# Even attention: probabilities times values as three products of high and low parts

## The chip, the cores and the metric

The kernel runs on one core of one Trainium2 chip. The metric is the device time of one execution in microseconds. Before the change it is 2157.37 us in the median of three runs (2157.3 to 2157.92).

## What is computed

The reference is one step of a two-layer trunk over 128 context and 512 latent tokens, with a width of 2048. Layer 0, the even one, has a windowed attention of 8 heads of 128 (two key and value heads) beside a gated linear attention (GLA); layer 1 has a neighbourhood attention beside a spatial gating. Each layer scales and shifts its input by a modulation that a conditioning vector gives, and adds its projected output through a gate. The change is in the latent tokens' attention of layer 0:

```python
s_band = einsum('bnqkgd,bnjkd->bnkgqj', qb, kb) * scale          # 3 blocks of 128 keys around a block
s_ctx = einsum('bnqkgd,blkd->bnkgql', qb, ck) * scale            # 128 cached keys
p = softmax(concatenate([s_band, s_ctx, sk], axis=-1), axis=-1)  # sk: a sink logit
...
o = einsum('bnkgqj,bnjkd->bnqkgd', pb, vb) + einsum('bnkgql,blkd->bnqkgd', pc, cv)
```

and in the modulation that the prediction speaks of:

```python
shift, scale, gate = split(silu(cond) @ ada_w[l] + ada_b[l], 3)
h = rms_norm(x, norm_g[l]) * (1.0 + scale) + shift
```

## The kernel before

**Tiling.** Activations lie with features on the 128 partitions, 16 tiles (k) of 640 tokens. A weight chunk of 128 output features is multiplied with all 16 tiles in two halves of the tokens (320 columns; 322 where two columns for the shift lie ahead). Weights and activations are split into a high part (fp32r, made by an ACT copy) and a low part (the rest, by a subtraction on POOL or DVE), and a product is three single-pass matmuls: high by high, low by high, high by low (`mm_k`). Small products (scores, transposes, probabilities by values, the GLA) are fp32 matmuls.

**Order.** The program is recorded by a planner. Its main list (`acts`) runs weight chunks; between matmuls `tick` (L454) advances tasks (generators such as `even_head`, L1389) whose inputs `Pace`, a model of the engines' times, holds to be ready. `Pace.record` (L138) books each instruction on its engine behind what it waits for. A low-priority task, `ada_task` (L1077), works off 640 reductions on DVE, each the product of 128 rows of a modulation matrix with the conditioning row: first 128 for the gate of layer 0, then 256 for scale and shift of layer 1 (written to `part`), and 256 half as long for the gate of layer 1 (to `partg`). `tick` adds one only where DVE, by the planner's clock, is not ahead of the present by more than `room` (0.3 us up to the end of the attention, then 1.5), and not in a `kpair` (L735) while any task is open. `need` lets the planner's time pass, without matmuls, until a flag is set.

**The stages around the change.** After the GLA, `open_att` (L1989) lays out the attention's buffers; then come chunks for k, v and q, and for each head a task `even_head`: rotary, five blocks of scores (`s1`), softmax (`soft1`, `soft2`), transposes of the probabilities and their copy from PSUM into `pT` (`s3`), and the product with the values into one bank. The attention's temporary buffers are parts of one tile, `arena`. `tok_major` (L1324) transposes the values. Gate chunks stand between heads. After the last head (`open_g0`, L2056) come two gate chunks, and the projection of layer 0 (`out_proj`, L2076). Its last two chunks are a `kpair`. After it `to_odd` (L2101) makes layer 1's input tile by tile: it waits for the flag `ada_1` that the 384th reduction sets. `rstd1` (L2119) makes the norm, and the main list has `need("shift1")` ahead of layer 1's first chunks.

## Time and profile before

| | |
|---|---|
| median of three runs | 2157.37 us |
| span of the profiled execution | 2155.7 us |
| TensorE busy, matmuls | 2099.9 us, 14326 |
| DVE busy | 1320.2 us |
| ACT busy | 907.2 us |
| POOL busy | 944.9 us |

The page has no own time of the profiled execution beside its span; the median lies 1.7 us above the span. Nearly all instructions go through helpers, so that lines tell little: matmuls have L371, transposes L376, and what DVE, ACT and POOL do has L205. Groups are told by the names and shapes of what they write and read. The attention runs from about 500 to 830 us, the projection of layer 0 from 883 to 1082 us, and layer 1 begins there.

### The profile page before, as it was taken

How to read it: one execution, taken by the hardware profiler on the slowest of the kernel's cores; microseconds unless marked ns; L12 is line 12 of the kernel's file. 1: busy time of each engine (PE TensorE's matmuls, PEld its weight loads, DVE VectorE, ACT ScalarE, POOL GpSimd, SP SyncE). 2: the span in 40 equal slices, each digit the busy share in tenths (PEclk: the TensorE clock that was granted, in tenths of full speed). 3: DMA queues.
4: the chain of work that ended last, by engine and by line, in shares of the span. 5: the costliest groups of instructions: out<-in, count | busy, mean ns of one | idle time of the engine just before them, and what ended most of it. 6: DMA issues, size and time to landing. Idle time of an engine off the chain costs nothing.

```text
span 2155.7 us, 38542 instructions
## 1 busy us (share of the span) xinstructions
PE 2099.9 (97%) x14326; PEld 2029.6 (94%) x14326; DVE 1320.2 (61%) x3190; ACT 907.2 (42%) x1962; POOL 944.9 (44%) x731
## 2 busy tenths in 40 slices
PE   7999999999999999999999999999999999999997
PEld 4789999999989999999999999999999999999996
DVE  1337787777777665889767887874344443354335
ACT  4435444343343444433464333444444453343333
POOL 3433333233223222566544455544444445536663
PEclk9999999999999999999999999999999999999998
DMA  9934433346435332577634345532222232233325
GB/s 374 365 136 153 133 103 105 105 126 192 124 98 165 128 123 81 193 226 220 212 99 127 119 139 163 185 103 79 89 78 78 88 134 80 80 109 122 105 93 193
DMA packets 161372, 303.08 MB, mean 141 GB/s; under 512 B 17376, under 2 KB 54048, under 8 KB 161184
## 3 DMA queue, kind: packets, MB, share of 16 engines
q1 hardware_dynamic: 159712, 299.06, 42.8%
q8 instruction: 112, 1.84, 0.3%
q10 hardware_dynamic: 1472, 1.56, 0.2%
q14 instruction: 76, 0.62, 0.1%
HBM read 278.52 MB, written 19.42 MB: 138 GB/s over the span
## 4 chain that ended last, share of the span: by engine, by line
PE 85%; DVE 5%; DMA 4%; issue 2%; POOL 2%; ACT 2%; SPq 0%; ACTq 0%; DVEq 0%; POOLq 0%
PE bank L371 82%; PE bank L376 2%; PE bank L1199 1%; DVE Y L205 1%; POOL wlo L205 1%; DMA rs<-w_out 1%; DVE arena L205 1%; DVE adas L205 1%; DMA adas<-ada 1%; ACT arena L205 1%; DVE bank L205 0%; ACT whi L205 0%; SPq L403 0%; DVE rs L205 0%; DMA crow<-crow 0%
## 5 line engine op out<-in xcount | busy, mean ns | idle before, releaser
L371 PE MATMUL bank<-acth,whi 128*128 128x320 f32 (+2 forms) x3592 | 1106.6, 318 | 18.2 <-DVE sums L205 8.8
L371 PE MATMUL bank<-acth,wlo 128*128 128x320 f32 (+2 forms) x3592 | 1078.6, 310 | 0.0
L371 PE MATMUL bank<-actl,whi 128*128 128x320 f32 (+2 forms) x3592 | 1077.3, 310 | 0.0
L205 POOL TENSOR_TENSOR wlo<-wraw,whi 128x512 fp32r<-128x512 f32 x375 | 504.2, 1348 | 724.2 <-ACT whi L205 634.0
L371 PEld LDWEIGHTS bank<-acth,whi 128*128 128x128 f32 (+1 forms) x3592 | 668.8, 189 | 35.5 <-DVE sums L205 10.3
L371 PEld LDWEIGHTS bank<-actl,whi 128*128 128x128 f32 (+1 forms) x3592 | 668.9, 189 | 1.5
L371 PEld LDWEIGHTS bank<-acth,wlo 128*128 128x128 f32 (+1 forms) x3592 | 668.4, 189 | 0.0
L205 POOL TENSOR_TENSOR wlo<-rs,whi 128x512 fp32r<-128x512 f32 x259 | 352.1, 1369 | 308.4 <-ACT whi L205 293.0
L205 ACT ACTIVATE whi<-wraw 128x512 fp32r<-128x512 f32 x383 | 237.0, 625 | 251.2 <-PE bank L371 116.0
L205 DVE TENSOR_TENSOR rs<-rs 128x512 f32<-128x512 f32 x148 | 155.2, 1050 | 134.0 <-DMA rs<-w_odd 57.8
L205 DVE CUSTOM_DVE_ANT_0 adas<-adas,bank,partg 128x256 bf16<-128x256 f32 (+1 forms) x320 | 178.6, 558 | 12.7 <-ACT bank L205 3.5
L205 ACT ACTIVATE whi<-rs 128x512 fp32r<-128x512 f32 x259 | 156.4, 621 | 27.3 <-PE bank L371 14.7
L205 DVE CUSTOM_DVE_ANT_0 adas<-adas,bank,part 128x512 bf16<-128x512 f32 x192 | 143.0, 745 | 9.7 <-ACT bank L205 3.6
L205 DVE TENSOR_TENSOR bank<-bank,sums 128x320 f32<-128x320 f32 (+1 forms) x148 | 72.4, 497 | 120.9 <-PE bank L371 120.2
L371 PE MATMUL bank<-eh,whi 128*128 128x322 f32 (+1 forms) x444 | 139.9, 315 | 0.0
L371 PE MATMUL bank<-el,whi 128*128 128x322 f32 (+1 forms) x444 | 137.6, 310 | 0.0
L371 PE MATMUL bank<-eh,wlo 128*128 128x322 f32 (+1 forms) x444 | 137.6, 310 | 0.0
L205 ACT ACTIVATE arena<-Y 128x320 f32<-128x320 f32 (+1 forms) x76 | 38.8, 512 | 172.7 <-DVE Y L205 152.8
L205 ACT ACTIVATE arena<-arena,bc 128x128 f32<-128x128 f32 (+4 forms) x171 | 84.9, 520 | 58.0 <-DVE arena L205 55.8
L205 ACT ACTIVATE bc<-bank 128x2 f32<-128x2 f32 (+1 forms) x101 | 17.2, 170 | 201.1 <-DVE arena L205 120.9
L205 POOL TENSOR_TENSOR arena<-arena 128x320 f32<-128x320 f32 x58 | 53.6, 924 | 103.8 <-ACT arena L205 103.2
L205 ACT ACTIVATE Y<-bank 128x128 f32<-128x128 f32 (+5 forms) x130 | 50.9, 410 | 110.4 <-PE bank L371 85.7
(159 smaller groups left out, 2215.5 us busy)
## 6 DMA issues: line engine op xcount, KB each, us to landing
wraw<-w_even SPq DMA_DIRECT2D x176, 256.0 KB, 3.2
adas<-ada_g SPq DMA_DIRECT2D x128, 256.0 KB, 3.7
adas<-ada SPq DMA_DIRECT2D x128, 256.0 KB, 3.6
wraw<-w_odd SPq DMA_DIRECT2D x124, 256.0 KB, 3.1
rs<-w_odd SPq DMA_DIRECT2D x50, 512.0 KB, 4.1
wraw<-w_out SPq DMA_DIRECT2D x88, 256.0 KB, 3.3
Y<-ada SPq DMA_DIRECT2D x37, 512.0 KB, 6.9
more<-ada SPq DMA_DIRECT2D x27, 512.0 KB, 7.1
```

The costliest lines, as they stand in the source:

```text
L205: return f(*args, **kw)
L371: self.nc.tensor.matmul(out, lhsT, rhs, start=start, stop=stop, **kw)
L376: self.nc.tensor.transpose(out, in_, self.ident[:k, :k])
L1199: nc.tensor.matmul(o, c, w[:, j, :], start=(q == 0), stop=(q == 3))
```

## The change

Probabilities and values are kept as high and low parts. ACT copies the transposed probabilities out of PSUM as fp32r (`pth`), and DVE subtracts that from PSUM for the low part (`ptl`); the values (`tok_halves`, in place of `tok_major`) and the cached values (`cvs`) are split in the same way. Each of the five fp32 products of a head becomes three single-pass products. The parts lie in tiles of their own in a pool `rv`; to make room, the arena shrinks, and some buffers move into tiles of `Y` that are not in use yet (`av`, `cos`). The flag `att` comes after the split of the cached values.

```diff
+    def tok_halves(self, src, ctx, hi, lo):
+        nc = self.nc
+        yield from self.until(src)
+        yield from self.bank()
+        p = self.sm()
+        r = p.rearrange("p (a b) -> p a b", b=128)
+        for i in range(4):
+            self.tr(r[:, i, :], src[:, 128 * i + 128 : 128 * i + 256])
+        nc.scalar.activation(hi, r, AF.Copy)
+        nc.vector.tensor_tensor(lo, r, hi.bitcast(F32), ALU.subtract)
+        yield from self.bank()
+        p = self.sm()
+        self.tr(p[:, 0:128], src[:, 0:128])
+        nc.scalar.activation(ctx, p[:, 0:128], AF.Copy)
...
-            o = pT[:, base : base + 256 * nb].rearrange("p (a b) -> p a b", b=256)[:, :, 0:128]
-            nc.vector.tensor_copy(o, pt[:, 0 : 128 * nb].rearrange("p (a b) -> p a b", b=128))
-            nc.scalar.activation(pT[:, 1536 + 128 * b : 1664 + 128 * b], pt[:, 128 * nb : 128 * nb + 128], AF.Copy)
+            r = pt[:, 0 : 128 * nb].rearrange("p (a b) -> p a b", b=128)
+            o, ol = (x[:, base : base + 256 * nb].rearrange("p (a b) -> p a b", b=256)[:, :, 0:128] for x in pT)
+            nc.scalar.activation(o, r, AF.Copy)
+            c, cl = (x[:, 1536 + 128 * b : 1664 + 128 * b] for x in pT)
+            rc = pt[:, 128 * nb : 128 * nb + 128]
+            nc.scalar.activation(c, rc, AF.Copy)
+            nc.vector.tensor_tensor(ol, r, o.bitcast(F32), ALU.subtract)
+            nc.vector.tensor_tensor(cl, rc, c.bitcast(F32), ALU.subtract)
...
-        self.mm(po, self.cv[:, kv, :], pT[:, 1536:2048], stop=False)
+        def three(o, w, x, st, sp):
+            for i, (a, b) in enumerate(((0, 0), (0, 1), (1, 0))):
+                self.mm(o, w[a], x[b], start=st and i == 0, stop=sp and i == 2)
+        three(po, [x[:, kv, :] for x in self.cvs], [x[:, 1536:2048] for x in pT], True, False)
         for j in range(4):
             b0, b1 = max(j - 1, 0), min(j + 2, 4)
             o0 = j * 384 + (b0 - j + 1) * 128
-            self.mm(
-                po[:, 128 * b0 : 128 * b1], vtok[:, 1 + j, :], pT[:, o0 : o0 + 128 * (b1 - b0)], start=False, stop=(j == 3)
+            three(
+                po[:, 128 * b0 : 128 * b1],
+                [x[:, j, :] for x in vhl],
+                [x[:, o0 : o0 + 128 * (b1 - b0)] for x in pT],
+                False,
+                j == 3,
             )
...
-            self.arena(17.5)
+            self.arena(12.0)
+            self.rp = tc.tile_pool(name="rv", bufs=1)
...
-            L["vtoks"] = Ring([Y[:, 7, :], self.take()])
+            vctx = self.take(256).rearrange("p (a b) -> p a b", b=128)
+            vhl = [self.t(rp, [128, 2, 4, 128], n, F32R) for n in ("vhi", "vlo")]
+            L["vtoks"] = [(vctx[:, kv, :], *(x[:, kv] for x in vhl)) for kv in range(2)]
...
-            self.pT = self.take(2048)
+            self.pT = [self.t(rp, [128, 2048], n, F32R) for n in ("pth", "ptl")]
+            self.cvs = [self.t(rp, [128, 2, 128], n, F32R) for n in ("cvh", "cvl")]
...
+                yield 3.0
+                yield from self.until(self.cv)
+                nc.scalar.activation(self.cvs[0], self.cv, AF.Copy)
+                nc.vector.tensor_tensor(self.cvs[1], self.cv, self.cvs[0].bitcast(F32), ALU.subtract)
                 self.flags.add("att")
...
+            self.flush()
+            self.rp.__exit__(None, None, None)
             self.close_arena()
```

The planner makes the whole order anew from there. Three places, each with the rows of before and then of the change:

On DVE, a block of the attention (`ISA` with `mx` is the row maximum of the next block's scores, `den` its softmax, `ISA adas,part` with its read a reduction of the low-priority task). Before, in one of the first heads:

```order
L205 COPY arena_4498<-bank_70 128x3x128
L205 ISA adas,part_99<-adas,bank_74 128x512
L205 ISA part_99 128x1
L205 TENSOR_TENSOR den_5115<-den_5115,es_5119 128x1
L205 RECIPROCAL den_5115<-den_5115 128x1
```

The last head with the change:

```order
L205 TENSOR_TENSOR ptl_4505<-bank_72,pth_4504 128x3x128
L205 TENSOR_TENSOR ptl_4505<-bank_72,pth_4504 128x128
L205 TENSOR_TENSOR den_7617<-den_7617,es_7622 128x1
L205 RECIPROCAL den_7617<-den_7617 128x1
L205 TENSOR_SCALAR arena_4498<-arena_4498,den_7617 128x512
L205 ISA arena_4498,mx_7664<-bank_70,arena_4498 128x384
```

The copy became two subtractions that read what ACT wrote (`pth`), and in many blocks the reduction behind it is gone. Of the 640 reductions, 270 stand ahead of the projection's first gated addition before, and 208 with the change.

On DVE, the end of the projection of layer 0 (`Y<-bank,G` is the gated addition that evacuates it, `A<-part` what the 384th reduction sets free, `actl<-Y` layer 1's input). Before, some 65 rows ahead of the projection's last gated addition:

```order
L205 ISA adas,part_99<-adas,bank_74,part_99 128x512
L205 ISA part_99 128x1
L205 TENSOR_TENSOR A_95<-part_99,b_92 128x16
L205 TENSOR_TENSOR A_95<-A_95,small 128x16
L205 TENSOR_TENSOR A_95<-part_99,b_92 128x16
L205 TENSOR_TENSOR A_95<-A_95,small 128x16
L205 TENSOR_TENSOR sums_7719<-sums_7719,bank_71 128x320
```

With the change, the last gated additions and what follows them:

```order
L205 SCALAR_TENSOR_TENSOR Y<-bank_68,G_96,arena_7788 128x128
L205 SCALAR_TENSOR_TENSOR Y<-bank_68,G_96,arena_7788 128x192
L205 SCALAR_TENSOR_TENSOR Y<-bank_69,G_96,arena_7788 128x320
L205 ISA adas,part_99<-adas,bank_73,part_99 128x512
L205 ISA part_99 128x1
```

and, after 46 more reductions and the eight instructions of the norm:

```order
L205 ISA adas,part_99<-adas,bank_74,part_99 128x512
L205 ISA part_99 128x1
L205 TENSOR_TENSOR A_95<-part_99,b_92 128x16
L205 TENSOR_TENSOR A_95<-A_95,small 128x16
L205 TENSOR_TENSOR A_95<-part_99,b_92 128x16
L205 TENSOR_TENSOR A_95<-A_95,small 128x16
L205 TENSOR_TENSOR part_99<-part_99,small 128x16 x2
L205 TENSOR_TENSOR actl<-Y,acth 128x640
```

The 384th reduction moved from the projection's middle to behind its last gated addition, and 48 reductions stand between that addition and layer 1's first input.

On TensorE, the step from the projection (320 columns in both halves) to layer 1 (322 in the first; `ones` is the norm's sum over the partitions). Before:

```order
L371 MATMUL bank_70<-acth,wlo 128x320
L371 MATMUL bank_67<-acth,wlo 128x320
L371 MATMUL bank_71<-acth,whi 128x322
L371 MATMUL bank_69<-acth,whi 128x320
L371 MATMUL bank_71<-actl,whi 128x322
```

With the change:

```order
L371 MATMUL bank_68<-acth,wlo 128x320
L371 MATMUL bank_69<-acth,wlo 128x320
L371 MATMUL bank_72<-arena_7788,ones 128x320 x2
L371 MATMUL bank_71<-acth,whi 128x322
L371 MATMUL bank_70<-acth,whi 128x320
```

In both, nothing but the norm's sums stands near the step; they moved ahead of layer 1's first matmul, which waits for the input that DVE writes.

## The prediction

> **What bounds the kernel now.** I read the busy table, the chain, the groups by shape, and then the timeline of each engine at the places that the new order of instructions moves.

> ```profile
> span 2155.7 us, 38542 instructions
> PE 2099.9 (97%) x14326; PEld 2029.6 (94%) x14326; DVE 1320.2 (61%) x3190; ACT 907.2 (42%) x1962; POOL 944.9 (44%) x731
> PE 85%; DVE 5%; DMA 4%; issue 2%; POOL 2%; ACT 2%; SPq 0%; ACTq 0%; DVEq 0%; POOLq 0%
> ```

> TensorE is busy for 97% of the span and carries 85% of the chain; 55.8 us of idle time are spread over the rest. So two things move the end: less time in TensorE's own instructions, and a place where TensorE comes to wait. Where it waits from 495 us on (the attention and two gates; then the projection of layer 0; then the step into layer 1), three answers of the view of waits tell (total us, times, longest):

> ```profile
> PE bank L376 <- DVE arena L205: 3.1, 3, 1.6
> PE bank L371 <- DVE arena L205: 2.2, 3, 1.3
> PE bank L376 <- ACT arena L205: 1.5, 1, 1.5
> PE bank L371 <- ACT bc L205: 0.8, 2, 0.7
> ...
> PE bank L371 <- DVE sums L205: 7.8, 5, 2.3
> ...
> PE bank L371 <- DVE Y L205: 2.4, 1, 2.4
> ```

> That is 7.6 us up to 880 us (the first four rows), 7.8 us in the projection and 2.4 us at the step into layer 1. All are small. The sum below is made against the span, 2155.7 us; the median of the runs is 1.7 us above it, and that difference is kept.

> **The products themselves.** One head's five fp32 products of probabilities and values stand in the timeline as ten records, since every fp32 matmul has two. The second row is a window: its length, the busy time and count of PE, PEld, DVE, ACT and POOL, the granted clock, the DMA share and rate:

> ```profile
> 742.33 3.17 PE L371 MATMUL bank<-arena 128*128 128x512 f32 x10
> 1200.00:1500.00 300.00, 300.00 (x2043) 296.55 (x2042) 223.94 (x650) 119.96 (x265) 149.73 (x112) 1.00 0.42 131
> L371 PE MATMUL bank<-acth,whi 128*128 128x320 f32 x2196 | 679.0, 316 | 13.5 <-DVE sums L205 8.8 <-DVE arena L205 2.6 <-ACT bc L205 1.9
> ```

> A record outlasts the start of its successor by about 0.16 us (316 ns long, one each 300/2043 us = 147 ns), so the ten take 3.17 - 0.16 = 3.01 us for 512+256+384+384+256 = 1792 columns. In single passes of the weights' kind a 320-column matmul comes every 147 ns, 0.459 ns a column; three passes over 1792 columns are 5376 columns, 2.47 us. A head saves 0.54 us, eight heads 4.3 us. From below: at half the time that a column of an fp32 record takes (3.01 us / 3584 / 2 = 0.42 ns) the three passes need 2.26 us, and 6.0 us are saved. From above: if none of the six passes of 256 columns goes under the 147 ns seen at 320, 2.64 us, and 3.0 us are saved. I take 4.3, nearest to the row of the same kind of matmul. [...]

> **What ACT and DVE get.** A block's transposed probabilities were copied by one DVE and one ACT instruction; now ACT copies both pieces and DVE subtracts both.

> ```profile
> L205 DVE COPY arena<-bank 128x128 f32<-128x128 f32 x10 | 2.9, 290 | 5.8 <-PE bank L376 5.8
> L205 ACT ACTIVATE arena<-bank 128x256 f32<-128x256 f32 x8 | 3.1, 384 | 22.0 <-PE bank L371 18.3 <-DMA o_state<-arena 3.8
> L205 ACT ACTIVATE arena<-bank 128x128 f32<-128x128 f32 x45 | 12.1, 270 | 15.4 <-DVE arena L205 15.3
> ```

> DVE gets some 0.29 us a block more (32 blocks, 9 us) and ACT 0.38 us or more (12 us or more). By busy time both have room. But DVE's subtraction now stands behind ACT's copy, and the order of the program is made with these waits in it: the reductions of the layer modulations on DVE, which are slipped in only where DVE is free, fall behind. Counted in the order of DVE's instructions, 270 of the 640 reductions stood ahead of the projection's first gated addition, and now 208. That is 62 fewer, 49 us of DVE time, for 9 us of added work.

> Within the attention this is a relief: the new order puts more weight matmuls between scores and transposes. Of the 7.6 us of waits there I take 3.0 away, somewhat under a half, since the new rows leave more room at most places but not at all (bounds 0 and 7.6). At its end, though, the last head's products now stand right behind its last transposes, with no weight matmul between, where before there were twelve (1.8 us). There TensorE waits for ACT's two copies, 0.38 + 0.27, and DVE's second subtraction, 0.29 and the passing between engines, some 0.6: 1.6 us (bounds 1 and 4).

> **The step into layer 1.** The 384th reduction completes layer 1's modulation, and no input of that layer can be scaled before it. It came early (the first row is a window with the instructions on the tile `adas` alone, on DVE the reductions):

> ```profile
> 883.00:1041.00 158.00, 0.00 (x0) 0.00 (x0) 84.72 (x114) 1.10 (x2) 0.00 (x0) 1.00 0.69 218
> 1040.42 0.75 DVE L205 CUSTOM_DVE_ANT_0 adas<-adas,bank,part 128x512 bf16<-128x512 f32 x1
> 1041.09 0.18 DVE L205 TENSOR_TENSOR A<-part,b 128x16 f32<-128x16 f32 x1
> ...
> 1082.11 0.45 PE L371 MATMUL bank<-acth,wlo 128*128 128x320 f32 x2
> 1082.40 0.46 PE L371 MATMUL bank<-acth,whi 128*128 128x322 f32 x2
> ```

> 114 reductions ran during the projection (270 to 384) and the last one at 1040.4 us, 42 us ahead of 1082.4, where TensorE went from the projection's last matmul to layer 1's first without a gap. In the new order the projection holds 128 reductions, up to the 336th. The last pair of the projection runs in a mode that admits none while other tasks are open, and one is open that waits for this very modulation. So the last **48** stand on DVE behind the projection's last evacuation, and layer 1's first inputs stand behind them. Each engine here takes its instructions in order, so all of that lies open: TensorE has nothing else. Its length, piece by piece:

> ```profile
> 1086.76 1.13 DVE L205 SCALAR_TENSOR_TENSOR Y<-bank,G,arena 128x128 f32<-128x128 f32 x3
> 667.09 0.74 DVE L205 CUSTOM_DVE_ANT_0 adas<-adas,bank,part 128x512 bf16<-128x512 f32 x1
> ...
> 675.12 0.49 DVE L205 TENSOR_TENSOR arena<-bank,rstd 128x320 f32<-128x320 f32 x1 [0.16 <-PE bank L371]
> ...
> 1095.05 0.48 DVE L205 TENSOR_SCALAR arena<-bank 128x320 f32<-128x320 f32 x1
> 1097.80 0.49 DVE L205 SCALAR_TENSOR_TENSOR arena<-rstd 128x320 f32<-128x320 f32 x1 [1.46 <-ACT rstd L205]
> 1100.24 0.48 DVE L205 TENSOR_SCALAR arena<-bank 128x320 f32<-128x320 f32 x1
> 1102.81 1.47 DVE L205 SCALAR_TENSOR_TENSOR rstd<-arena,rstd 128x320 f32<-128x320 f32 x1
> 1041.31 1.22 DVE L205 TENSOR_TENSOR A<-A,small 128x16 f32<-128x16 f32 x1
> 1060.23 1.00 ACT L205 ACTIVATE Y<-Y,A 128x128 f32<-128x128 f32 x2
> 1062.00 1.00 ACT L205 ACTIVATE Y<-Y,A 128x128 f32<-128x128 f32 x2
> 1062.78 0.15 DVE L205 SCALAR_TENSOR_TENSOR actl<-part,acth 128x2 fp32r<-128x2 f32 x1
> ```

> - the last evacuation, 1.13 us and the drain of the matmul ahead of it: 1.5 us;
> - ten reductions with their reads run from 667.09 to 674.96 us (0.16 us before the next row), 0.787 us each: 48 take 37.8 us;
> - the norm's chain, in the new order between the reductions: its first half from 1095.05 to 1100.3 us, 5.3 us (ACT's part sets it); its second from 1100.24 to 1104.3 us, 4.0 us, of which one reduction fills 0.8: 8.5 us;
> - scale and shift: before, 2.6 us from 1041.1 to 1043.7, with 1.2 us for 16 columns beside a working POOL; the small subtractions and additions without that, 1.5 us;
> - the first input: 1060.23 to 1062.93 us, 2.7 us, and the start of the matmul, 2.8 us.

> Together 52.1 us, less the 2.4 us that TensorE waited there anyhow: **+49.7 us** (46 to 54, by scale and shift, and by how far the norm's wait is filled).

> Then TensorE starts cold and its inputs come one by one:

> ```profile
> 2145.00:2150.00 5.00, 0.00 (x0) 0.00 (x0) 5.00 (x11) 0.00 (x0) 4.06 (x5) 0.50 0.64 223
> 20.00:30.00 10.00, 7.65 (x60) 4.38 (x60) 1.58 (x5) 4.11 (x9) 6.76 (x6) 0.83 1.04 401
> ```

> After a pause the granted clock is 0.50 (2145 to 2150 us, no matmul), and in 20 to 30 us it was 0.83 on average, 3.4 us at half: 1.7 us of work lost. Inputs come every 1.8 us (1060.23 to 1062.00) where TensorE uses 12 matmuls of 147 ns, 1.8 us; only the second is late, by 0.9. Together 2.6 us (bounds 0 and 5). The projection's 7.8 us of waits I leave as they are, since nearly as many reductions stand in it as before (128 for 123, nine of these half as long): bounds -4 and +3.

> **The sum.** -4.3 -3.0 +1.6 +49.7 +2.6 = +46.6 us. A span of 2202.3 us, and 2157.4 + 46.6 = **2204.0 us**.

> **The rivals.**
> - *The relief is larger.* DVE loses 49 us of reductions from the attention. If all 7.6 us of waits went there and half of the projection's, and the products saved 6.0, the time would be 2204.0 - 4.6 - 3.9 - 1.7 = 2193.8, and with the open stretch at its shortest (46) 2190.1. For it: every wait there names DVE or ACT. Against: the projection's DVE load stays.
> - *The reductions run at the pace of their loads.* 256 KB are loaded for each pair, and the trace has a stretch in which the loads and the row copies set the pace:

> ```profile
> 645.44 0.68 DVE L205 CUSTOM_DVE_ANT_0 adas<-adas,bank 128x512 bf16<-128x512 f32 x1
> 659.31 0.75 DVE L205 CUSTOM_DVE_ANT_0 adas<-adas,bank,part 128x512 bf16<-128x512 f32 x1 [1.40 <-DMA adas<-ada]
> 662.36 0.49 DVE L205 TENSOR_TENSOR arena<-bank,rstd 128x320 f32<-128x320 f32 x1
> ...
> adas<-ada SPq DMA_DIRECT2D x128, 256.0 KB, 3.6
> ```

>   16 in 16.9 us, 1.06 each; 48 would take 50.8, 13.0 more: 2217. Against it: a load has three pairs, 4.7 us, from its issue to its use, and lands after 3.6 in the median; no row copy falls among the 48.
> - *Faster: only the products count.* If DVE reached the 48 reductions while TensorE still works on the projection's last pair (192 matmuls of 147 ns, 28 us) and the spans before it, the open stretch would shrink to nothing once some 38 us of them got ahead of the evacuation, and 2157.4 - 4.3 - 3.0 = 2150.1 us would remain. Against it: an evacuation that waits for TensorE stands ahead of them, and DVE waits in order:

> ```profile
> 1055.87 0.25 DVE L205 TENSOR_TENSOR part<-part,small 128x16 f32<-128x16 f32 x2
> ...
> 1079.89 0.83 DVE L205 TENSOR_TENSOR actl<-Y,acth 128x640 fp32r<-128x640 f32 x1 [5.04 <-ACT acth L205]
> ...
> 1080.70 0.16 DVE L205 TENSOR_TENSOR fsh<-part 128x2 f32<-128x2 f32 x1
> ```

>   It stood idle for 5.04 us before 1079.89 us, though the subtraction at 1080.70 us needs nothing but the finished shift of 1056 us. [...]

> **How the numbers follow.** The stall as worked out 0.74 (2196 to 2212), the larger relief 0.10 (2187 to 2196), the loads' pace 0.11 (2212 to 2220), the faster rival 0.05, of which 0.02 within 0.2%. The range 2190 to 2217 leaves out the last and the outer halves of the two others. 0.2% is 4.3 us, about what a measurement of this kernel can tell from no change: slower 0.95, within 0.02, faster 0.03.

> **What would show it.** The step into layer 1 shows as one idle time of TensorE of about 50 us, with a granted clock near a half, DVE full of reductions in it; the products' fifteen records take about 2.5 us a head; before the projection TensorE idles less, but for the last head. No such idle time, or one under 40 us, would prove the main step wrong; a busy DVE with gaps named after loads, the second rival.

## The result

The changed kernel takes **2220.5 us** (median of four runs, 2219.4 to 2221.4), against 2157.4 us before (2157.3 to 2157.9): **+63.1 us**, a ratio of 1.0291 with a 95% interval from 1.0276 to 1.0305. Forecast were 2204.0 us with a range from 2190 to 2217. The direction and the main mechanism came as forecast; the size lies 3.5 us outside the range. Of the ten executions of one run below (the one with DVE first, a median of 2162.9 us), one took 3431.4 us at a granted clock of 0.56 and is left out of its ratio.

### The profile page after: what moved, and what is told of

Its sections match the earlier page's. It is cut to its first block, busy times and chain, and to the rows that moved or that the text cites. A ratio compares the mean times of both kernels' runs of the same rounds, so it can differ in the third digit from the quotient of the medians.

```text
span 2217.2 us, 38696 instructions
## 1 busy us (share of the span) xinstructions
PE 2106.3 (95%) x14366; PEld 2040.5 (92%) x14366; DVE 1344.3 (61%) x3225; ACT 919.9 (41%) x1997; POOL 949.5 (43%) x731
## 4 chain that ended last, share of the span: by engine, by line
PE 80%; DVE 7%; DMA 4%; ACT 3%; issue 3%; POOL 2%; SPq 0%; ACTq 0%; DVEq 0%; POOLq 0%
PE bank L371 76%; PE bank L376 2%; DVE adas L205 2%; DVE arena L205 2%; POOL wlo L205 1%; PE bank L1199 1%; DVE Y L205 1%; DMA rs<-w_out 1%; ACT arena L205 1%; DMA adas<-ada 1%; ACT acth L205 1%; ACT whi L205 1%; DVE bank L205 0%; DVE actl L205 0%; DVE rs L205 0%
## 5 line engine op out<-in xcount | busy, mean ns | idle before, releaser
L371 PE MATMUL bank<-acth,whi 128*128 128x320 f32 (+2 forms) x3592 | 1107.0, 318 | 59.2 <-ACT acth L205 42.8
L371 PE MATMUL bank<-actl,whi 128*128 128x320 f32 (+2 forms) x3592 | 1079.9, 311 | 1.2 <-DVE actl L205 1.1
L371 PE MATMUL bank<-acth,wlo 128*128 128x320 f32 (+2 forms) x3592 | 1080.2, 311 | 0.0
L205 POOL TENSOR_TENSOR wlo<-wraw,whi 128x512 fp32r<-128x512 f32 x375 | 507.8, 1359 | 786.6 <-ACT whi L205 715.4
L371 PEld LDWEIGHTS bank<-acth,whi 128*128 128x128 f32 (+1 forms) x3592 | 670.3, 189 | 77.2 <-ACT acth L205 44.4
L371 PEld LDWEIGHTS bank<-actl,whi 128*128 128x128 f32 (+1 forms) x3592 | 670.1, 189 | 4.1 <-DVE actl L205 2.7
L371 PEld LDWEIGHTS bank<-acth,wlo 128*128 128x128 f32 (+1 forms) x3592 | 670.0, 189 | 0.0
L205 POOL TENSOR_TENSOR wlo<-rs,whi 128x512 fp32r<-128x512 f32 x259 | 352.4, 1371 | 303.5 <-ACT whi L205 292.6
L205 ACT ACTIVATE whi<-wraw 128x512 fp32r<-128x512 f32 x383 | 236.6, 625 | 251.7 <-PE bank L371 129.4
L205 DVE TENSOR_TENSOR rs<-rs 128x512 f32<-128x512 f32 x148 | 164.3, 1111 | 126.7 <-DMA rs<-w_odd 52.1
L205 DVE CUSTOM_DVE_ANT_0 adas<-adas,bank,partg 128x256 bf16<-128x256 f32 (+1 forms) x320 | 178.6, 558 | 15.2 <-ACT bank L205 6.5
L205 ACT ACTIVATE whi<-rs 128x512 fp32r<-128x512 f32 x259 | 156.8, 621 | 24.8 <-PE bank L371 14.2
L205 DVE CUSTOM_DVE_ANT_0 adas<-adas,bank,part 128x512 bf16<-128x512 f32 x192 | 143.1, 745 | 9.3 <-DMA adas<-ada 4.3
L205 DVE TENSOR_TENSOR bank<-bank,sums 128x320 f32<-128x320 f32 (+1 forms) x148 | 72.3, 497 | 121.6 <-PE bank L371 121.4
L371 PE MATMUL bank<-eh,whi 128*128 128x322 f32 (+1 forms) x444 | 140.0, 315 | 0.0
L371 PE MATMUL bank<-eh,wlo 128*128 128x322 f32 (+1 forms) x444 | 137.7, 310 | 0.7 <-POOL wlo L205 0.7
L371 PE MATMUL bank<-el,whi 128*128 128x322 f32 (+1 forms) x444 | 137.7, 310 | 0.0
L205 ACT ACTIVATE arena<-Y 128x320 f32<-128x320 f32 (+1 forms) x76 | 38.8, 511 | 169.8 <-DVE Y L205 151.3
L205 ACT ACTIVATE arena<-arena,bc 128x128 f32<-128x128 f32 (+4 forms) x167 | 82.4, 518 | 52.8 <-DVE arena L205 50.7
L205 ACT ACTIVATE bc<-bank 128x2 f32<-128x2 f32 (+1 forms) x101 | 17.1, 170 | 198.5 <-DVE arena L205 121.2
L205 POOL TENSOR_TENSOR arena<-arena 128x320 f32<-128x320 f32 x58 | 54.1, 933 | 102.8 <-ACT arena L205 102.8
L205 ACT ACTIVATE Y<-bank 128x128 f32<-128x128 f32 (+5 forms) x128 | 50.1, 409 | 109.8 <-PE bank L371 87.1
## 6 DMA issues: line engine op xcount, KB each, us to landing
wraw<-w_even SPq DMA_DIRECT2D x176, 256.0 KB, 3.3
adas<-ada_g SPq DMA_DIRECT2D x128, 256.0 KB, 3.8
adas<-ada SPq DMA_DIRECT2D x128, 256.0 KB, 3.6
wraw<-w_odd SPq DMA_DIRECT2D x124, 256.0 KB, 3.2
wraw<-w_out SPq DMA_DIRECT2D x88, 256.0 KB, 3.3
```

Source lines behind the costliest of these rows:

```text
L205: return f(*args, **kw)
L371: self.nc.tensor.matmul(out, lhsT, rhs, start=start, stop=stop, **kw)
```

## The profile after

The page's head, busy times and chain:

```profile
span 2217.2 us, 38696 instructions
PE 2106.3 (95%) x14366; PEld 2040.5 (92%) x14366; DVE 1344.3 (61%) x3225; ACT 919.9 (41%) x1997; POOL 949.5 (43%) x731
PE 80%; DVE 7%; DMA 4%; ACT 3%; issue 3%; POOL 2%; SPq 0%; ACTq 0%; DVEq 0%; POOLq 0%
```

The span grew by 61.5 us, TensorE's busy time by 6.4 only. The rest is idle time, and DVE's and ACT's shares of the chain rose.

**Where on the way.** TensorE's timeline at four places that both kernels have, the changed one first (start, duration, instruction, idle time before it and what ended that). Of the kernel before, the two rows that the prediction doesn't show follow:

```profile
871.00 0.41 PE L371 MATMUL bank<-acth,whi 128*128 128x320 f32 x1 [1.29 <-DVE arena L205]
1096.06 0.45 PE L371 MATMUL bank<-acth,wlo 128*128 128x320 f32 x2
1144.71 0.90 PE L371 MATMUL bank<-acth,whi 128*128 128x322 f32 x2 [42.18 <-ACT acth L205]
1805.89 0.41 PE L371 MATMUL bank<-acth,whi 128*128 128x320 f32 x1 [0.97 <-DVE sums L205]
```

```profile
858.68 0.41 PE L371 MATMUL bank<-acth,whi 128*128 128x320 f32 x1 [1.29 <-DVE arena L205]
1744.34 0.41 PE L371 MATMUL bank<-acth,whi 128*128 128x320 f32 x1 [0.97 <-DVE sums L205]
```

A gate behind the attention comes 12.3 us later. The projection's last matmuls come at 1096.06 where they came at 1082.11 us: 13.95 later, so the projection adds 1.6. Layer 1's first matmul comes at 1144.71 where it came at 1082.40, and deep in layer 1 the distance is 61.55 us: the step with its restart adds 47.6. (The medians are 1.6 us further apart than this, since the profiled execution of the changed kernel, 2219.36 us, was the fastest of its four.)

**The step into layer 1.** The group of the reductions from 1097 to 1145 us (busy, mean ns of one, idle time before them), some of DVE's rows there, and the window in which TensorE restarts (columns as in the prediction: PE, PEld, DVE, ACT, POOL, granted clock, DMA):

```profile
L205 DVE CUSTOM_DVE_ANT_0 adas<-adas,bank,part 128x512 bf16<-128x512 f32 x48 | 35.9, 747 | 1.6
```

```profile
1097.46 0.74 DVE L205 CUSTOM_DVE_ANT_0 adas<-adas,bank,part 128x512 bf16<-128x512 f32 x1
...
1099.82 0.75 DVE L205 CUSTOM_DVE_ANT_0 adas<-adas,bank,part 128x512 bf16<-128x512 f32 x1
1100.49 0.49 DVE L205 TENSOR_SCALAR arena<-bank 128x320 f32<-128x320 f32 x1
1102.62 0.49 DVE L205 SCALAR_TENSOR_TENSOR arena<-rstd 128x320 f32<-128x320 f32 x1 [1.64 <-ACT rstd L205]
...
1140.30 0.75 DVE L205 CUSTOM_DVE_ANT_0 adas<-adas,bank,part 128x512 bf16<-128x512 f32 x1
1140.97 0.17 DVE L205 TENSOR_TENSOR A<-part,b 128x16 f32<-128x16 f32 x1
```

```profile
1144.70:1150.20 5.50, 5.49 (x18) 4.75 (x19) 2.88 (x7) 5.40 (x14) 0.00 (x0) 0.50 0.00 0
```

All 48 reductions stand there, back to back, and with 1.6 us of idle time ahead of them in all (33 ns each) none waits for a load. From TensorE's last matmul, about 1096.5, to its first of layer 1 are 48.2 us (a few short matmuls of the norm lie in it). Then it runs 5.5 us at half clock.

**The attention.** TensorE's waits from 495 to 880 us (total us, times, longest):

```profile
PE bank L376 <- DVE arena L205: 8.2, 5, 3.8
PE bank L371 <- ACT pth L205: 4.1, 1, 4.1
PE bank L376 <- ACT Y L205: 2.6, 1, 2.6
PE bank L371 <- DVE arena L205: 1.3, 1, 1.3
PE bank L371 <- ACT bc L205: 0.8, 2, 0.7
```

That is 17.0 us, where the same view had 7.8 before (the prediction's 7.6, and 0.2 in a row that it left out). And each of the longer waits is followed by 3.4 us or more at half clock. The first row below is a window of the kernel before, the others are of the changed one: three stretches, the same one among them, and what follows the waits of 2.2 and 4.1 us:

```profile
560.00:620.00 60.00, 58.23 (x377) 53.63 (x376) 47.12 (x138) 23.00 (x68) 14.09 (x11) 1.00 0.33 98
```

```profile
495.00:560.00 65.00, 62.17 (x411) 61.28 (x410) 46.03 (x122) 22.22 (x46) 20.51 (x16) 0.97 0.58 185
560.00:620.00 60.00, 53.19 (x340) 51.80 (x339) 39.55 (x109) 23.68 (x71) 12.66 (x9) 0.91 0.24 74
720.00:860.00 140.00, 135.27 (x915) 133.21 (x914) 80.12 (x201) 69.03 (x154) 41.78 (x30) 0.99 0.28 87
576.80:580.20 3.40, 3.40 (x14) 3.40 (x15) 2.38 (x8) 1.30 (x7) 0.00 (x0) 0.50 0.46 160
832.70:836.10 3.40, 3.38 (x10) 2.81 (x11) 3.29 (x10) 1.01 (x2) 2.51 (x2) 0.51 0.05 14
```

So a wait there costs more than its length. Of the four longest, two name DVE and one ACT's copies (`pth`). DVE's idle time from 495 to 860 us has a first row that the kernel before doesn't have; below it is the row of the kernel before for the same place, where DVE copied the probabilities itself:

```profile
DVE ptl L205 <- ACT pth L205: 48.5, 30, 2.3
```

```profile
DVE arena L205 <- PE bank L376: 19.4, 29, 2.5
```

For 48.5 us DVE stood idle until ACT's copies of the probabilities were done, in 30 of 32 blocks. Not all of that is ACT's: the row names only what came last, and before, DVE waited 19.4 us there for the transposes alone. ACT's place ahead of DVE adds some 30 us. How that reaches TensorE shows in one block:

```profile
596.90 0.22 DVE L205 TENSOR_SCALAR nm<-mx,sink 128x1 f32<-128x1 f32 x1
597.15 0.72 ACT L205 ACTIVATE arena<-arena,nm 128x512 f32<-128x512 f32 x1 [3.94 <-DVE nm L205]
597.88 0.28 ACT L205 ACTIVATE es<-nm,sink 128x1 f32<-128x1 f32 x1
598.37 0.66 ACT L205 ACTIVATE pth<-bank 128x384 fp32r<-128x384 f32 x2 [0.22 <-PE bank L376]
599.06 0.76 DVE L205 TENSOR_TENSOR ptl<-bank,pth 128x384 fp32r<-128x384 f32 x2 [1.94 <-ACT pth L205]
599.74 0.15 DVE L205 TENSOR_TENSOR den<-den,es 128x1 f32<-128x1 f32 x1
600.12 0.49 DVE L205 TENSOR_SCALAR arena<-arena,den 128x512 f32<-128x512 f32 x1
600.66 0.66 PE L376 MATMUL bank<-ident,arena 128*128 128x128 f32 x4 [0.76 <-DVE arena L205]
```

The copies (`pth`) and subtractions (`ptl`) belong to the block ahead, the rest to the block whose softmax is running. Its exponentials are done at 598.16, but its sum and scaling (`den`) stand on DVE behind the subtractions, and these behind ACT's copies, which stand behind this block's exponentials and start when the transposes of the block ahead are done (0.22 us later). From the maximum (`nm`) to the scaling are 3.2 us, and TensorE comes to the transposes too early.

A second thing lengthens DVE's part in some blocks. The addition to `den`, one number a partition, takes 0.15 us in the block above. In the next one it takes 1.17 us beside a subtraction of POOL:

```profile
603.39 1.26 POOL L205 TENSOR_TENSOR wlo<-wraw,whi 128x512 fp32r<-128x512 f32 x1 [8.46 <-ACT whi L205]
603.50 1.17 DVE L205 TENSOR_TENSOR den<-den,es 128x1 f32<-128x1 f32 x1
```

In the changed kernel 16 of the 40 additions take 1.1 to 1.2 us, each of them while POOL works; in the kernel before it is 5 of 40 (0.8 to 1.3 us). Two of the 16, at 574.86 and 603.50 us, stand right ahead of the waits of 2.2 and 3.8 us. In the rows shown both stand behind ACT's copies: DVE's through the subtractions, POOL's through the `whi` that ACT makes right after them (at 602.69 us).

**The products.** The first of a head's fifteen records, and the matmul behind them:

```profile
762.65 0.39 PE L371 MATMUL bank<-pth,cvh 128*128 128x512 f32 x1
...
765.11 0.31 PE L371 MATMUL bank<-acth,whi 128*128 128x322 f32 x1
```

2.46 us, for 3.01 before. In the last head they take 4.24 us, since they follow the wait of 4.1 us.

## The experiments

Theory: the elementwise work of the split sets the loss, in two ways. The late reductions stall the step (48 us), and DVE's place behind ACT's copies delays the softmax in the attention and pushes the reductions out. The products themselves only gain. Rivals: the products or the new tiles delay the attention; the stall comes from something else at the step; it is the amount of DVE's work that counts and not where it waits. A run's time is its median; ratios are to the kernel before on the same chip. `room` is the allowance of the filler task `ada_task`.

**One half of the change at a time.** The products without subtractions, and the copies and subtractions without the three passes:

```diff
-            nc.scalar.activation(o, r, AF.Copy)
+            nc.vector.tensor_copy(o, r)
...
-            nc.vector.tensor_tensor(ol, r, o.bitcast(F32), ALU.subtract)
-            nc.vector.tensor_tensor(cl, rc, c.bitcast(F32), ALU.subtract)
...
-        three(po, [x[:, kv, :] for x in self.cvs], [x[:, 1536:2048] for x in pT], True, False)
+        three(po, [x[:, kv, :] for x in self.cvs], [pT[0][:, 1536:2048]]*2, True, False)
```

> The products alone: probabilities are copied as before (one DVE and one ACT copy a block) into single-pass operands, nothing is subtracted, and the three passes use the high part twice (the low parts of the probabilities are left out). In its order 389 reductions stand ahead of the projection's last gated addition, none of layer 1's late. If the elementwise work does the harm, the stall at the step into layer 1 is gone and the attention waits stay near the 7.6 us of before: 2157.4 - 4.3 = 2153 us (2148 to 2160). If the products themselves, or the new tiles and values' split, make the attention wait (16.9 us of idle time and four more stretches at half clock in the changed kernel), some 12 us of that remain: 2165 us.

```diff
         def three(o, w, x, st, sp):
-            for i, (a, b) in enumerate(((0, 0), (0, 1), (1, 0))):
-                self.mm(o, w[a], x[b], start=st and i == 0, stop=sp and i == 2)
+            self.mm(o, w[0].bitcast(F32), x[0].bitcast(F32), start=st, stop=sp)
```

> The copies and subtractions alone: the order of the changed kernel to the instruction, but each product is one fp32 matmul of the high parts (ten records instead of fifteen; the low parts are made and left out of the product). If the three passes save 0.56 us a head, this is the changed kernel plus 4.5: 2225 us, with the same stall of 48 us. If the waits of the last head hide a part, 2222 us. If the three passes save nothing where they stand, 2220.5 us.

The products alone took 2153.2 us, a ratio of 0.9976 (0.9966 to 0.9987): faster than before, by what the products save. Neither the three passes nor the new tiles delay anything that shows (attention's waits 8.2 us). The copies alone took 2223.2 us, 1.0298 (1.0282 to 1.0314), the changed kernel's loss without its gain. The difference between the two runs with the same order, 2.7 us, is under the 4.5 expected and within their intervals; in the profile the gain is there behind the last product (837.1 us against 841.8), and the projection's waits give it back. The changed kernel first:

```profile
PE bank L371 <- DVE sums L205: 8.5, 5, 2.3
```

```profile
PE bank L371 <- DVE sums L205: 4.2, 4, 2.3
```

There TensorE waits for DVE, and where it comes earlier it waits longer.

**The number of late reductions.** Three ways to have fewer of them behind the projection:

```diff
-    rooms, calms, lags = (0.3, 1.5), (4.0, 2.0), (3.0, 3.0, 2.0, 1.0, 0.4)
+    rooms, calms, lags = (0.6, 1.5), (4.0, 2.0), (3.0, 3.0, 2.0, 1.0, 0.4)
```

> The changed kernel, but the filler task may book a reduction while DVE is booked up to 0.6 us ahead instead of 0.3 (until the projection). 368 reductions stand ahead of the projection's last gated addition, 16 of layer 1's stand late instead of 48. If the stall is the late reductions in single file, 32 fewer take 32 x 0.787 = 25.2 us from it: 2220.5 - 25 = 2195 us (2189 to 2202). If the stall is set by something else (the norm's chain, the loads), it stays near 48 us: 2215 to 2221 us. If more reductions in the attention lengthen the waits there by what they take from the stall, 2205 to 2221.

The same line with 1.0:

> The changed kernel with that allowance at 1.0 us: 417 reductions ahead of the projection's last gated addition, none of layer 1's late. If the stall is the late reductions, it goes altogether with its cold start: 2220.5 - 48 - 2.7 = 2170 us (2164 to 2176), and what then stays over the kernel before, about 12 us, is the attention's waits and half clock. If reductions moved into the attention cost there what they save later, 2185 us or more.

And the filler task let into the projection's last pair (`last` is true from ahead of that pair to behind it):

```diff
-            if self.low and not (self.quiet and self.tasks) and self.low[0] <= self.now and self.pace.t["v"] <= self.now + self.room:
+            if self.low and not (self.quiet and self.tasks and not self.last) and self.low[0] <= self.now and self.pace.t["v"] <= self.now + self.room:
```

> The changed kernel, but the filler task may also book reductions while the projection's last pair runs. The order up to that pair is that of the changed kernel; 364 reductions stand ahead of the projection's last gated addition instead of 336, so 20 of layer 1's stand late instead of 48. If the late reductions set the stall: 28 x 0.787 = 22 us less, 2198.5 us (2194 to 2203), with the attention's waits unchanged at 15 us. If the reductions delay the evacuations of the last pairs by as much, 2210 to 2220.

They took 2199.8, 2187.2 and 2201.0 us (ratios 1.0196, 1.0137 and 1.0203, each within 0.0017). The longest wait at the step of each, with 16, no and 20 reductions late, went from 42.18 us to the first row below (allowance 0.6), to none (with 1.0 only the 2.4 us of before are left) and to the second (last pair):

```profile
PE bank L371 <- ACT acth L205: 17.7, 2, 16.8
```

```profile
PE bank L371 <- ACT acth L205: 19.4, 2, 18.8
```

The stall is the late reductions: 32 fewer shorten all waits at the step from 45.5 to 22.7 us, 0.71 each. But allowance 1.0 brought only 33 of the 50 us expected, because the reductions cost something where they went. TensorE's waits from 495 to 880 us with it:

```profile
PE bank L376 <- DVE arena L205: 18.2, 8, 4.4
PE bank L371 <- DVE arena L205: 4.7, 3, 2.9
PE bank L371 <- ACT bc L205: 3.8, 1, 3.8
```

28.1 us in all with a fourth and a fifth row, for 17.0, and a granted clock of 0.96 on average there, for 0.98. The run with the last pair, whose order up to there is that of the changed kernel, kept 17.4 us in the attention; its 19.5 us of gain are near the 22 expected.

**What delays the attention: DVE's work, or its place behind ACT.** First the wait on ACT's result was to go:

```diff
-            nc.vector.tensor_tensor(ol, r, o.bitcast(F32), ALU.subtract)
-            nc.vector.tensor_tensor(cl, rc, c.bitcast(F32), ALU.subtract)
+            nc.vector.tensor_scalar(ol, r, 0.0, None, ALU.mult)
+            nc.vector.tensor_scalar(cl, rc, 0.0, None, ALU.mult)
```

> The changed kernel with each subtraction replaced by a DVE instruction of the same size on the same bank that does not read ACT's copy (it writes zero, so the low parts of the probabilities are left out). DVE has the same work and no wait for ACT; 332 reductions stand ahead of the last gated addition, 52 late. If the attention's waits (15.1 us of idle time from 495 us to the last head's products, 17 us at half clock) come from DVE waiting for ACT in its queue, they fall to some 6 us as in the run of the products alone, and with four more late reductions (+3) the time is 2220.5 - 9 - 5 + 3 = 2209 us (2205 to 2214). If they come from DVE's work itself, the time is 2220 to 2226 us.

It took 2223.0 us (1.0303, 1.0286 to 1.0319), which looks like the verdict "work". It is none, since the wait did not go. DVE's idle time in that run:

```profile
DVE ptl L205 <- ACT pth L205: 49.6, 29, 2.7
```

DVE's instruction takes nothing from ACT any more, but it reads the bank that ACT's copies read and stands behind them, and in the trace the two engines read that bank one after the other: in 29 of 32 blocks DVE's idle time ahead of it ends with ACT's copies, 49.6 us in all. So whoever reads the bank second would wait, whatever it reads from the other. Two runs change who is second: one with all four instructions of the change on DVE, one with the four of the last run in another order:

```diff
-            nc.scalar.activation(o, r, AF.Copy)
+            nc.vector.tensor_copy(o, r)
...
-            nc.scalar.activation(c, rc, AF.Copy)
+            nc.vector.tensor_copy(c, rc)
             nc.vector.tensor_tensor(ol, r, o.bitcast(F32), ALU.subtract)
             nc.vector.tensor_tensor(cl, rc, c.bitcast(F32), ALU.subtract)
```

> The changed kernel with both copies of the probabilities on DVE ahead of its two subtractions: more work for DVE (two copies a block, some 0.6 us), no instruction of ACT in the chain. 350 reductions stand ahead of the last gated addition, 34 late instead of 48: 11 us less of the stall. If the wait for ACT makes the attention wait, another 9 to 14 us go: 2196 to 2201. If DVE's work does, the waits there grow by as much as the work behind the last transposes, and the time is 2210 us or more.

```diff
-            nc.scalar.activation(o, r, AF.Copy)
...
-            nc.scalar.activation(c, rc, AF.Copy)
-            nc.vector.tensor_tensor(ol, r, o.bitcast(F32), ALU.subtract)
-            nc.vector.tensor_tensor(cl, rc, c.bitcast(F32), ALU.subtract)
+            nc.vector.tensor_scalar(ol, r, 0.0, None, ALU.mult)
+            nc.vector.tensor_scalar(cl, rc, 0.0, None, ALU.mult)
+            nc.scalar.activation(o, r, AF.Copy)
+            nc.scalar.activation(c, rc, AF.Copy)
```

> The instructions of the run without the read of ACT's copy (DVE writes zero instead of the low parts, which are left out), but DVE's two stand ahead of ACT's two copies, so that ACT waits for DVE at the shared bank and DVE no longer for ACT. In the changed kernel and in that run DVE sat idle for 48.5 and 49.6 us behind ACT's copies. DVE's work is the same; 382 reductions stand ahead of the projection's last gated addition, 2 late. If DVE's place behind ACT is what pushes the reductions out and delays the attention: attention's waits near 8 us, some 10 us of wait at the step (two reductions and the norm), 2157.4 - 4.3 + 8 + 3 + 2 = 2166 us (2160 to 2171). If DVE's work, or ACT's two copies as such, delay the attention, its waits stay at 15 us with their half clock: 2178 us.

With everything on DVE: 2199.9 us (1.0197, 1.0180 to 1.0214), though DVE has two copies a block more to do; the attention's waits fall to 10.6 us. With DVE first: **2162.9 us** (1.0021, 1.0012 to 1.0031), as expected from the place behind ACT, with the same instructions as the run of 2223.0 us. (The changed kernel can't use this order as it stands, since its low parts are made from ACT's copies.) DVE's idle time and then TensorE's waits from 495 to 880 us (the longest two):

```profile
DVE ptl L205 <- PE bank L376: 18.9, 28, 2.0
```

```profile
PE bank L376 <- ACT Y L205: 2.6, 1, 2.6
PE bank L371 <- DVE arena L205: 2.3, 2, 1.3
```

DVE now waits for the transposes alone, about as long as the 19.4 us of before. The block of above, in this run:

```profile
592.39 0.21 DVE L205 TENSOR_SCALAR nm<-mx,sink 128x1 f32<-128x1 f32 x1
592.63 0.76 DVE L205 TENSOR_SCALAR ptl<-bank 128x384 fp32r<-128x384 f32 x2
...
593.90 0.15 DVE L205 TENSOR_TENSOR den<-den,es 128x1 f32<-128x1 f32 x1
594.29 0.49 DVE L205 TENSOR_SCALAR arena<-arena,den 128x512 f32<-128x512 f32 x1
```

DVE's two instructions run while ACT makes the exponentials; from the maximum to the scaling are 1.9 us, not 3.2, and another instruction of 0.68 us (left out) still lies between. And the order of the program, made with these times, has 382 reductions ahead of the projection's last gated addition instead of 332.

**Versions to use.** All three products with both copies on DVE and enough allowance, and two versions with fewer passes:

> The full three products with both copies and both subtractions on DVE, allowance 0.7 us: 391 reductions ahead of the last gated addition, none late. From the run with DVE's copies alone (2199.9 us, 36.0 us of wait at the step): 2199.9 - 33.6 - 2.7 = 2163.6 us if the 41 reductions more that stand ahead of it cost nothing there; with the price seen from allowance 0.6 to 1.0 (49 reductions more, 9.7 us more of waits up to the last head's products) 2172 us. Faster than the kernel before only if the attention's waits fall below 6 us, which neither theory gives.

```diff
-            for i, (a, b) in enumerate(((0, 0), (0, 1), (1, 0))):
-                self.mm(o, w[a], x[b], start=st and i == 0, stop=sp and i == 2)
+            for i, (a, b) in enumerate(((0, 0), (1, 0))):
+                self.mm(o, w[a], x[b], start=st and i == 0, stop=sp and i == 1)
```

(with the probabilities' copies of the run of the products alone, and `room` 0.4)

> Two passes (high and low part of the values, high part of the probabilities; the low parts of the probabilities are left out), probabilities copied as before with nothing subtracted, allowance 0.4 us so that 389 reductions stand ahead of the projection's last gated addition and none late. Ten passes of 1792 columns a head: 1.65 us instead of 3.01, eight heads 10.9 us: 2157.4 - 10.9 = 2146.5 us (2142 to 2151) if the elementwise work is all that harms. If shorter products leave TensorE waiting for the next scores, 2150 to 2158.

> The two-pass kernel once more with five rounds, beside the one-pass kernel on one chip: 2148 us (2144 to 2150), ratio to the kernel before 0.9956 as in its first run.

The same with the pair `(0, 0)` alone, and `room` 0.5:

> One pass a product (high part of the probabilities times high part of the values; both low parts are left out of it), probabilities copied as before, nothing subtracted there, allowance 0.5 us: 402 reductions ahead, none late. Five passes of 1792 columns take 0.82 us a head instead of 3.01: 17.5 us, 2157.4 - 17.5 = 2140 us (2135 to 2148) if TensorE's time is what counts; if the attention is paced by DVE and ACT by now, little of the 6.6 us between one and two passes arrives: 2146 to 2149 us.

The full version took 2169.2 us (1.0054, 1.0038 to 1.0069), still more than the kernel before: the stall is gone, and the attention's waits, 19.5 us, are what remains. Two passes took 2148.2 and, again, 2150.4 us (0.9956, 0.9941 to 0.9971; 0.9968, 0.9956 to 0.9979), one pass 2148.7 us (0.9956, 0.9942 to 0.9969). Both beat both kernels, but leave out low parts; whether these can be spared is a question of the accuracy wanted. One pass came out no faster than two: its five records take 0.8 us, as expected, but TensorE waits 13.3 us from 495 to 880 us instead of 9.3. But that doesn't show that DVE and ACT pace the attention, as one of its expectations had it, since the two runs differ in the allowance too (0.5 and 0.4). The first row of TensorE's waits with one pass:

```profile
PE bank L371 <- ACT bc L205: 5.7, 2, 5.0
```

The wait of 5.0 us, at 502.7 us, is for ACT to read a chunk's shift (`bc`) out of its bank, ahead of the attention's first scores. All four runs with an allowance of 0.5 or more have it there, 3.8 to 5.0 us long; in all the others no wait for `bc` is over 0.7 us. Without it one pass would wait 8.3 us. That wait is most of the 6.6 us that one pass less was to save, and one pass with 0.4 was not run.

All runs together; the waits are sums of the view of TensorE's waits from 495 to 880 us, and of its idle times from the projection's last matmul to some 60 us on; "late" counts the reductions of layer 1 behind the projection's last gated addition:

| run | late | attention's waits, us | clock 495 to 880 | waits at the step, us | time, us |
|---|---|---|---|---|---|
| before | 0 | 7.8 | 1.00 | 2.4 | 2157.4 |
| changed | 48 | 17.0 | 0.98 | 45.5 | 2220.5 |
| products alone | 0 | 8.2 | 1.00 | 2.4 | 2153.2 |
| copies alone | 48 | 17.4 | 0.98 | 46.3 | 2223.2 |
| allowance 0.6 | 16 | 20.5 | 0.96 | 22.7 | 2199.8 |
| allowance 1.0 | 0 | 28.1 | 0.96 | 2.4 | 2187.2 |
| into the last pair | 20 | 17.4 | 0.97 | 27.1 | 2201.0 |
| DVE's zero, ACT first | 52 | 17.9 | 0.97 | 47.8 | 2223.0 |
| DVE's zero, DVE first | 2 | 8.7 | 0.99 | 8.4 | 2162.9 |
| both copies on DVE | 34 | 10.6 | 0.99 | 36.0 | 2199.9 |
| the same, allowance 0.7 | 0 | 19.5 | 0.97 | 2.4 | 2169.2 |
| two passes | 0 | 9.5, 9.3 | 1.00, 0.99 | 2.4 | 2148.2, 2150.4 |
| one pass | 0 | 13.3 | 0.98 | 2.9 | 2148.7 |

## Why the prediction was right in kind and too low

- **The products** (-4.3): right. 0.55 us a head, and the run of the products alone is 4.0 us faster than before. No run shows the 6.0 us of the bound from below and of the larger relief, which halve the time that a column of an fp32 record takes: 2.46 us a head for 3.01 are 4.4 us in eight heads.
- **The step** (+49.7, of which 2.4 as a deduction): right in its mechanism, some 4 us too much. The stretch took 48.2 us for 52.1 worked out. The 48 reductions took what was said: from 1097.46 to 1140.97 us are 43.5, less 5.8 for the norm between them, 37.7 us for 37.8. The norm was over-sized (8.5): four reductions filled the first half's wait for ACT.
- **The restart** (+2.6): about right. Behind 1144.71 us the net is +1.6, that is 47.6 less the 46.0 of the step (48.4 between the first matmuls of layer 1, without the 2.4 of before).
- **The attention** (-3.0 for relief, +1.6 for the last head): **this is the step that failed.** With the products it was to bring the gates 5.7 us forward; they came 12.3 us later, 18 us off, which is more than the whole miss. The prediction took some of DVE's reductions out of the attention, called that "a relief", and priced the subtraction "behind ACT's copy" only by what it does to the reductions. The same place in the queue delays each block's sum and scaling: TensorE's waits went from 7.8 to 17.0 us, where some 6 were forecast. DVE was less busy there (39.6 us of 560 to 620, for 47.1) and TensorE waited more, so a relief in busy time was the wrong measure.
- **Half clock in the attention** was left out, though the prediction priced it at the step. The clocks of 0.97, 0.91 and 0.99 in the windows 495 to 560, 560 to 620 and 720 to 860 us are 2.0 + 5.4 + 1.4 = 8.8 us of work lost; before, all three are 1.00 (its one stretch at half clock, 1.7 us of work, lies behind them from 859.3 us).
- **The last head** (+1.6, bounds 1 and 4): the wait was 4.1 us, and its products lost 1.8 us more at half clock. ACT's copies stood behind a gate chunk's activations (a table load of 1.28 us among them). The 0.6 us for the passing between engines was the author's estimate; in the block shown above it is 0.03 us from ACT's copies to DVE's subtraction and 0.05 us from DVE's scaling to TensorE.
- **The projection** (0, bounds -4 and +3): +1.6, within its bounds.

Against the sum that is 18.0 us more up to the gates, 1.6 more in the projection, 3.7 less at the step and 1.0 less behind it; with the 1.6 us by which the medians lie further apart than the profiles, it makes the 16.5 us between 2204.0 and 2220.5.

The rivals: the larger relief was the wrong way round. The loads' pace didn't come: DVE's idle time ahead of the 48 reductions is 1.6 us in all. The faster rival, reductions overtaking the wait, didn't come, as argued: DVE stood idle for 23.18 us ahead of a gated addition at 1093.75 us, with all 48 reductions behind it. And for each engine, the trace of the kernel before has the instructions in the program's order: TensorE's 14326 records, DVE's 2469, ACT's 1854 and POOL's 723 instructions (reads of accumulators, table loads and memsets aside). The range failed since none of its cases had an attention that gets slower.

How the reductions came to be displaced, which the prediction told as the order being "made with these waits in it", is shown by the two runs with the same instructions: DVE second at the bank leaves 332 reductions ahead, DVE first 382. `Pace.record` sets DVE's clock to the end of an instruction with its wait, so while DVE waits `tick` finds no room for a reduction.

What stays open: whether the price of a reduction inside the attention (allowance 0.6 to 1.0: 49 more ahead of the last gated addition, 7.6 us more waits) comes from their length on DVE or from where the planner puts them; no run separates these. For the step from 0.3 to 0.6 one place can be named: with 0.6 TensorE waits 2.9 us at 497 us and 4.1 us at 507 us, ahead of the first scores, where the changed kernel has no such waits. Open is also what the long additions beside POOL cost. With DVE first there are 3 of them; with everything on DVE 15, and yet the attention waits 10.6 us only. So they are not the whole of it, and no run takes them out alone.

## What to carry to other kernels

When work moves from one engine to two, look first at who reads the shared bank second and what is queued behind that instruction; here the order of two readers was worth 60 us (2223.0 to 2162.9) with the same instructions, 39 of them in the stall (47.8 to 8.4 us). A busy share that falls is no relief where the engine's idle time is a wait in its queue. And filler work that loses its slots doesn't vanish: count where it goes, and price it at the place where something waits for it.

## What the runs showed of the hardware

```profile
573.34:576.75 3.41, 1.22 (x9) 0.95 (x7) 3.34 (x5) 0.00 (x0) 2.72 (x2) 1.00 0.50 147
```

```profile
575.71:579.12 3.41, 1.58 (x12) 1.58 (x13) 2.71 (x6) 0.55 (x2) 1.11 (x1) 1.00 0.56 180
```

TensorE was idle for 2.19 us of the first and 1.83 us of the second. Counted in the traces of the kernel before and of the changed one, from 100 us on to 30 us before the end, over the windows that ran at full clock: each of the 8 with 1.96 to 3.38 us idle was followed by half clock, and none of the others, which were idle for 1.73 us at the most. Nor is it always one long wait: in the kernel before, 0.66 and 1.29 us in one window, 1.96 us idle in all, were followed by half clock from 859.33 us.
